# Recurrent gates of a hybrid encoder layer: the array's rows hold one head's high and low part, its columns both gates

## The chip, the cores and the metric

The kernel runs on one core of a Trainium2 chip. The metric is the device time of one execution in microseconds (us), taken as the median of several executions of the same program. A profiled execution gives the trace; its span is the time from the first to the last recorded instruction.

## The reference, cut to what matters

One encoder layer is applied to two sequences of width 1024: a prompt of 512 rows and a sample of 1024 rows. After a LayerNorm the input is multiplied by `w_in` and split into four parts of 512 channels: convolution value and gate, recurrent input and gate. The recurrent half is the part that changes. In each of two directions a depthwise convolution of width 4 gives x, and x goes through a gated linear recurrence with 8 heads of 64 channels:

```python
xh = x.reshape(bsz, seq, RNN_HEADS, RNN_HEAD_DIM)             # 8 heads of 64
gate_a = einsum("bshi,hij->bshj", xh, w_a) + b_a               # 64 x 64 per head
gate_x = einsum("bshi,hij->bshj", xh, w_x) + b_x
r, i = sigmoid(gate_a), sigmoid(gate_x)
log_a = -8 * r * softplus(-lam)
a = exp(log_a);  b = sqrt(-expm1(2 * log_a)) * (i * x)
h[t] = a[t] * h[t-1] + b[t]                                    # or backwards
```

The two directions are added and multiplied by gelu of the recurrent gate. The convolution half is a depthwise convolution of width 31 with a LayerNorm and a swish. Both halves go through `w_out`, a residual and a LayerNorm, and then through a ConvFFN (up to 2 x 2816 channels, convolution of width 3, gelu gate, down to 1024) with a second residual and LayerNorm.

## The kernel before, in words

**Arithmetic.** Every large product is made of three matmuls. An operand is kept as a high part, its rounded copy in the reduced format that the array takes (fp32r), and a low part, the rest. `prod3` (L534) lists the three pairs: high x high, high x low, low x high. `split` (L489) makes the two parts: ScalarE copies the high part, and a second engine (VectorE or GpSimd) subtracts it from the input.

**Layout.** The recurrent channels lie on the 128 partitions in four groups j, two heads in each: head 2j on partitions 0 to 63, head 2j+1 on partitions 64 to 127. A tile of work is 128 channels by 512 columns of time.

**One recurrent chain** is one group j, one direction d and one block of 512 columns (`chain`, L844, for the sample; the loop in `mixer_p`, L777 to L782, for the prompt). It runs `conv4` (one activation and three multiply-adds), `split` with the low part on GpSimd, `rg_gates` (L722), `rg_decay` (L731: five activations with three changes of the activation table, and multiply-adds) and `scan` (L746). In `rg_gates` the weight tile of a gate is a 128 x 128 matrix with the two heads' 64 x 64 blocks on its diagonal and zeros elsewhere. For each of the two gates three matmuls of 128 x 128 by 512 columns go into one PSUM bank, and ScalarE takes a sigmoid of the whole bank; then VectorE multiplies the second gate by x. The banks come from a ring of two.

**Stages and their order.** In the order of the program: LayerNorm and `w_in` of the prompt; `w_in_s`, the same for the sample (16 weight tiles, 48 matmuls each); `mixer_p`, both halves of the prompt's mixer; the prompt's `residual` (192 matmuls with `w_out`) and `ln1`; `mixer_s(1)` and the prompt's `ffn`; then `residual`, `ln1`, `mixer_s(0)` and `ffn(1)` of the second half of the sample; then the same for its first half. `mixer_p` has 8 chains, `mixer_s(1)` 12 (its forward scan runs over both blocks), `mixer_s(0)` 4.

**What sets the order.** The kernel first lists its operations with a cost, a priority and what they depend on. `plan` (L274) simulates the five engines and picks, at each step, the ready operation of the lowest priority number; `look` lets it take an operation that becomes ready within so many ns, `pen` is added to an activation that changes the table. It knows a port that GpSimd and two-input VectorE operations share. `emit` (L356) makes one plan for each entry of `PLANS` (L377) and writes the instructions of every engine in the order of the plan with the shortest end. So every engine has one fixed order, and stages overlap: `w_in_s` (priority 30) fills TensorE beside `mixer_p` (13 to 16), and an `ffn` fills it beside `mixer_s`.

The parameters of the gates are columns of one tile `par` (`C_BA`, `C_BX`, L32 to L34), and the weights are laid out on the host in `layouts` (L1128).

Of the kernel before, what the change touches and what calls it, by code (L numbers as in the profile page):

```python
# [11 lines left out]
AF = mybir.ActivationFunctionType  # L12
ALU = mybir.AluOpType
# [17 lines left out]
C_RB = C_RW + 32  # L31
C_BA = C_RB + 8  # L32
C_BX = C_BA + 8
C_LAM = C_BX + 8  # L34
C_FW = C_LAM + 8
C_FB = C_FW + 3 * 2 * NPAIR
NPAR = C_FB + 2 * NPAIR
# [7 lines left out]
class View:  # L45
# [13 lines left out]
    @property  # L59
    def f32(self):  # L60
        return self._with(lambda a: a.bitcast(F32)) if self.buf.dtype != F32 else self

    @property
    def rev(self):
# [309 lines left out]
                    mybir.DependencyClass.Sync, mybir.DependencyReason.DATA), reason="port")  # L374


PLANS = [(60, 3.0, 0.0, 0), (160, 3.0, 0.0, 0), (160, 8.0, 0.0, 0), (260, 3.0, 0.0, 0)]  # L377


def body(ctx, tc, xp, xs, w_in, gw, w_out, w_up, w_down, par, gb, out_p, out_s):  # L380
# [3 lines left out]
    S = Sched(tc, sb, ps)  # L384
# [23 lines left out]
    col = lambda c: P[c:c + 1]  # L408
# [80 lines left out]
    def split(hi, lo, src, prio, hi_eng="act", lo_eng="dve"):  # L489
        S.copy(hi_eng, hi, src, prio)  # L490
        S.tt(lo_eng, lo, src, hi.f32, ALU.subtract, prio)
# [42 lines left out]
    def prod3(wh, wl, xh, xl):  # L534
        return [(wh, xh), (wh, xl), (wl, xh)]
# [92 lines left out]
    gwt = S.buf("GW", [2, 2, 4, 128], f32r), S.buf("GB", [2, 2, 4, 128], f32r)  # L628
# [35 lines left out]
    def decays():  # L664
# [3 lines left out]
        d = S.buf("sv", [8])  # L668
        lam = P[C_LAM:C_LAM + 8]
        pr = 12  # L670
# [39 lines left out]
    def conv4(src, dst, d, j, n, prio, t0=0, N=None):  # L710
        N = N or n
        order = (3, 2, 1, 0) if d == 0 else (0, 1, 2, 3)
        for i, k in enumerate(order):
# [4 lines left out]
            else:  # L718
                lo, hi = max(t0, -sh), min(t0 + n, N - sh)
                S.stt(dst(lo - t0, hi - t0), src(lo + sh, hi + sh), c, dst(lo - t0, hi - t0), ALU.mult, ALU.add, prio)  # L720

    def rg_gates(xf, hl, r, d, j, banks, prio):  # L722


        for ax, cb in ((0, C_BA), (1, C_BX)):
            bk = S.buf(banks(), [512], psum=True)
            S.mm(bk.all, prod3(gwt[0][d, ax, j], gwt[1][d, ax, j], *hl), True, True, prio)
            S.act(r if ax == 0 else bk.all, bk.all, AF.Sigmoid, 1.0, col(cb + d * 4 + j), prio)
        S.tt("dve", xf, bk.all, xf, ALU.mult, prio)

    def rg_decay(xf, r, q, st, d, j, prio, eng):  # L731

# [33 lines left out]
    def mixer_p():  # L766
        bk = rot(["M2", "M3"])
        acc = S.buf("T3", [4, 512])
        for j, bank in enumerate(("C0", "U2", "U3", "C1")):
            pc = S.buf(bank, [512], psum=True)  # L770
            conv31(lambda a, b: p_c[j, a:b], lambda a, b: pc[a:b], j, 512, 16)
            S.copy("act", acc[j], pc.all, 15)
        for j in range(4):
            t0 = S.buf("T0", [2, 2, 512])
            t1 = S.buf("T1", [2, 2, 512])
            hl = S.buf("G3", [2, 2, 512], f32r)
            for d in range(2):  # L777
                conv4(lambda a, b: p_rx[j, a:b], lambda a, b, d=d: t0[0, d, a:b], d, j, 512, 14)
                split(hl[0, d], hl[1, d], t0[0, d], 14, lo_eng="pool")
                rg_gates(t0[0, d], (hl[0, d], hl[1, d]), t0[1, d], d, j, bk, 14)  # L780
                rg_decay(t0[0, d], t0[1, d], t1[0, d], t1[1, d], d, j, 14, "pool")
                scan(t1[0, d], t0[1, d], t0[0, d], d, 14)  # L782
            S.tt("dve", t1[0, 0], t1[0, 0], t1[0, 1], ALU.add, 14)
            S.tt("dve", t1[0, 0], t1[0, 0], p_ge[j], ALU.mult, 14)
            split(xcP[0][1][j], xcP[1][1][j], t1[0, 0], 14)
        z = S.buf("G1", [4, 512])
        for tt in range(4):
            conv_norm(lambda j: acc[j, tt * 128:(tt + 1) * 128], [(0, 4, z[tt])], tt, "c", bk, 13)
        c = S.buf("T3", [4, 512])
        for j in range(4):  # L790
            b = S.buf(bk(), [512], psum=True)
            S.transposes([(b[tt * 128:(tt + 1) * 128], z[tt, j * 128:(j + 1) * 128]) for tt in range(4)], b.all,
                         idn.all, 13)
            S.act(c[j], b.all, AF.Silu, col(C_CG + j), col(C_CBB + j), 13)
            split(xcP[0][0][j], xcP[1][0][j], c[j], 13)
    mixer_p()


# [45 lines left out]
    def chain(rx, c, hl, d, j, t0, carry, bk, prio):  # L844

        conv4(rx, lambda a, b: c[0, a:b], d, j, 512, prio, t0, N)
        split(hl[0], hl[1], c[0], prio, lo_eng="pool")
        rg_gates(c[0], (hl[0], hl[1]), c[1], d, j, bk, prio)
        rg_decay(c[0], c[1], c[2], c[3], d, j, prio, "pool")
        if carry is not None:  # L850
            e = slice(0, 1) if d == 0 else slice(511, 512)
            S.stt(c[0, e], c[1, e], carry, c[0, e], ALU.mult, ALU.add, prio)
        scan(c[2], c[1], c[0], d, prio)
# [229 lines left out]
    for i in range(4):  # L1083
        for nh in range(2):
            b = S.buf(names(), [512], psum=True)
# [9 lines left out]
        if i == 0:  # L1095
            for nh in range(2):
                b = S.buf(names(), [512], psum=True)
                c = slice(nh * 512, (nh + 1) * 512)
# [9 lines left out]
    q = slice(768, 1024)  # L1108
# [4 lines left out]
    for nh in range(2):  # L1113
        n = 512 - 256 * nh
        v, c = last[nh - 2][0:n], slice(nh * 512, nh * 512 + n)
        x = y0[1][1, c]
        S.stt(v, v, mean, g2(c), ALU.subtract, ALU.mult, 5)
        S.stt(x, v, rstd, b2(c), ALU.mult, ALU.add, 5)
        c = slice(nh * 512, nh * 512 + 512)
        x = y0[1][1, c]  # L1120
# [7 lines left out]
def layouts(i):  # L1128

    c = np.ascontiguousarray  # L1130
    g = {k: np.asarray(v) for k, v in i.items()}
    w_in = c(g["w_in"][0].reshape(8, 128, 16, 128).transpose(2, 1, 0, 3)).reshape(16, 128, 1024)
    w_up = c(g["w_up"][0].reshape(8, 128, 44, 128).transpose(2, 1, 0, 3)).reshape(44, 128, 1024)
    w_out = c(g["w_out"][0].reshape(4, 2, 128, 2, 512).transpose(3, 0, 2, 1, 4)).reshape(2, 4, 128, 1024)
    w_down = c(g["w_down"][0].reshape(22, 128, 1024))
    gw = np.zeros((2, 2, 4, 128, 128), np.float32)
    for ax, n in enumerate(("rg_w_a", "rg_w_x")):
        for d in range(2):
            for h in range(8):
                j, o = divmod(h, 2)  # L1140
                gw[d, ax, j, o * 64:o * 64 + 64, o * 64:o * 64 + 64] = g[n][0, d, h]
    gw = c(gw.transpose(3, 0, 1, 2, 4)).reshape(128, 2048)
    ch = lambda a: a.reshape(-1, 128).T
    par = np.concatenate([
        c(g["conv_dw_w"][0].reshape(CW, 4, 128).transpose(2, 1, 0)).reshape(128, 4 * CW),
        ch(g["conv_dw_b"][0]), ch(g["conv_ln_g"][0]), ch(g["conv_ln_b"][0]),
        ch(g["rnn_conv_w"][0]), ch(g["rnn_conv_b"][0]), ch(g["rg_b_a"][0]), ch(g["rg_b_x"][0]), ch(g["rg_lambda"][0]),
        c(g["ffn_dw_w"][0].reshape(3, 44, 128).transpose(2, 1, 0)).reshape(128, 132), ch(g["ffn_dw_b"][0])], axis=1)
    gb = np.stack([g["ln_in_g"], g["ln_in_b"], g["ln1_g"][0], g["ln1_b"][0], g["ln2_g"][0], g["ln2_b"][0]])
    return {"xp": c(g["x_prompt"][0]), "xs": c(g["x_sample"][0]), "w_in": w_in, "gw": gw, "w_out": w_out, "w_up": w_up,  # L1150
            "w_down": w_down, "par": c(par), "gb": c(gb)}
# [15 lines left out]
```

## Time and profile before

| | before |
|---|---|
| median of 3 executions (lowest to highest) | 1571.3 us (1571.17 to 1571.7) |
| the profiled execution's own time | 1571.57 us |
| its span | 1569.6 us |
| TensorE busy / weight loads busy | 1543.7 us (98%) / 1280.2 us (82%) |
| VectorE busy | 1150.9 us (73%) |
| ScalarE busy | 825.2 us (53%) |
| GpSimd busy | 166.6 us (11%) |
| granted TensorE clock | 0.998 of full speed |

Busy time is the time in which at least one instruction of the engine is open. Matmuls are pipelined and overlap in the record, so a matmul's mean of 390 ns is not what it costs in a row of matmuls; that is read from how many of them start in a stretch of time. PE is TensorE, PEld its weight loads, DVE VectorE, ACT ScalarE, POOL GpSimd and SP the queue that issues the transfers.

### The profile page before, as it was taken

To read this page: it belongs to the slowest core of one execution; us is meant where nothing else is said; L and a number is where in the kernel's file an instruction comes from. 1 tells how busy PE (TensorE), PEld (TensorE's weight loads), DVE (VectorE), ACT (ScalarE), POOL (GpSimd) and SP (SyncE) were. 2 spreads that over 40 slices of the span, in tenths; PEclk is the share of its full clock that TensorE was granted. 3 is DMA by queue.
4 is the path that set the end of the run, shared out by engine and by line. 5 is a ranking of instruction groups with operands and counts; after the bars stand their busy time and mean duration, and the time that the engine had idled before them with its cause. 6 is when DMAs were issued, how large, how long until landed. Compare 5 with 4: busy or idle time off the path is not lost.

```text
span 1569.6 us, 19146 instructions
## 1 busy us (share of the span) xinstructions
PE 1543.7 (98%) x7036; PEld 1280.2 (82%) x7036; DVE 1150.9 (73%) x1849; ACT 825.2 (53%) x1031; POOL 166.6 (11%) x186
## 2 busy tenths in 40 slices
PE   6999999999999999999999999999999999999997
PEld 6888888888887888888887888888888888888885
DVE  8999974589999999653889988744438644545367
ACT  4647885249888883633369634352423433334351
POOL 3101111001211221100211000000002000000003
PEclk9999999999999999999999999999999999999999
DMA  9954337357565467666675766575675666565641
GB/s 375 328 181 139 108 121 239 130 191 227 166 225 183 154 230 234 208 223 220 202 257 181 277 205 210 168 244 191 210 249 184 201 199 199 195 198 178 200 159 67
DMA packets 107661, 316.09 MB, mean 201 GB/s; under 512 B 11952, under 2 KB 12080, under 8 KB 107440
## 3 DMA queue, kind: packets, MB, share of 16 engines
q1 hardware_dynamic: 107568, 314.88, 60.2%
q8 instruction: 55, 0.90, 0.2%
q14 instruction: 38, 0.31, 0.1%
HBM read 247.72 MB, written 67.11 MB: 201 GB/s over the span
## 4 chain that ended last, share of the span: by engine, by line
PE 80%; DVE 11%; ACT 5%; DMA 2%; issue 2%; POOL 0%; SPq 0%; DVEq 0%; ACTq 0%
PE b L262 78%; DVE b L208 7%; ACT b L240 4%; DVE b L199 3%; ACT L240 2%; PE b L270 2%; DMA b<-mixs_d 1%; DVE b L749 0%; DMA lo_up_d<-b 0%; DMA b<-gb 0%; DVE b L430 0%; DMA lo_down_d<-b 0%; POOL b L199 0%; SPq L251 0%; POOL b L222 0%
## 5 line engine op out<-in xcount | busy, mean ns | idle before, releaser
L262 PE MATMUL b<-b,b 128*128 128x512 f32 (+1 forms) x6748 | 1519.2, 386 | 4.3 <-DVE b L199 2.5
L262 PEld LDWEIGHTS b<-b,b 128*128 128x128 f32 x6748 | 1246.7, 188 | 261.7 <-DVE b L199 5.1
L208 DVE SCALAR_TENSOR_TENSOR b<-b,b,b 128x512 f32<-128x512 f32 (+14 forms) x848 | 569.2, 701 | 180.6 <-ACT b L240 167.2
L240 ACT ACTIVATE b<-b 128x1024 fp32r<-128x1024 f32 (+4 forms) x576 | 445.0, 798 | 437.5 <-PE b L262 210.2
L199 DVE TENSOR_TENSOR b<-b,b 128x512 f32<-128x512 f32 (+6 forms) x494 | 394.0, 817 | 144.0 <-ACT b L240 80.7
L240 ACT ACTIVATE b<-b,b 128x512 f32<-128x512 f32 (+2 forms) x346 | 261.3, 775 | 277.6 <-PE b L262 204.6
L199 POOL TENSOR_TENSOR b<-b,b 128x1 f32<-128x1 f32 (+4 forms) x84 | 89.8, 1077 | 1010.0 <-DVE b L222 407.9
L240 ACT ACT_TABLE_LOAD x109 | 139.8, 1283 | 23.5 <-DVE b L208 14.0
L199 POOL TENSOR_TENSOR b<-b 128x512 f32<-128x512 f32 (+1 forms) x47 | 60.8, 1297 | 379.2 <-ACT b L240 190.8
L208 DVE SCALAR_TENSOR_TENSOR b<-b,b 128x512 f32<-128x512 f32 (+2 forms) x81 | 50.8, 640 | 59.9 <-PE b L262 54.6
L430 DVE BATCH_NORM_STATS2 b<-b 128x6 f32<-128x512 f32 x84 | 55.9, 683 | 6.0 <-DMA b<-xp 4.5
L199 DVE TENSOR_TENSOR b<-b 128x1 f32<-128x1 f32 (+3 forms) x85 | 43.2, 525 | 21.2 <-ACT b L240 20.9
L270 PE MATMUL b<-b,b 128*128 128x128 f32 x288 | 39.9, 281 | 11.4 <-DVE b L208 11.4
L208 DVE SCALAR_TENSOR_TENSOR b<-b 128x512 f32<-128x512 f32 (+1 forms) x73 | 48.4, 676 | 0.6 <-ACT b L240 0.5
L270 PEld LDWEIGHTS b<-b,b 128*128 128x128 f32 x288 | 34.8, 145 | 17.1 <-issue 10.9
L749 DVE TENSOR_TENSOR_SCAN b<-b 128x512 f32<-128x512 f32 x24 | 29.1, 1217 | 0.1
L222 POOL TENSOR_SCALAR b<-b 128x1 f32<-128x1 f32 x36 | 15.3, 430 | 7.9 <-DVE b L208 2.3
L222 DVE TENSOR_SCALAR b<-b 128x1 f32<-128x1 f32 (+1 forms) x60 | 8.9, 153 | 1.4 <-POOL b L199 0.9
L432 DVE BATCH_NORM_AGGREGATE b<-b 128x2 f32<-128x12 f32 (+1 forms) x48 | 9.2, 196 | 0.3
L247 DVE COPY b<-b 128x2 f32<-128x2 f32 x44 | 6.6, 150 | 0.0
L222 DVE TENSOR_SCALAR b<-b,b 128x512 f32<-128x512 f32 x2 | 0.9, 483 | 0.0
L437 DVE RECIPROCAL b<-b 128x1 f32<-128x1 f32 x4 | 0.5, 154 | 0.4 <-ACT b L240 0.4
(14 smaller groups left out, 2.2 us busy)
## 6 DMA issues: line engine op xcount, KB each, us to landing
b<-w_up SPq DMA_DIRECT2D x132, 512.0 KB, 4.5
b<-lo_up_d SPq DMA_DIRECT2D x88, 512.0 KB, 4.1
b<-w_down SPq DMA_DIRECT2D x132, 256.0 KB, 4.2
lo_up_d<-b SPq DMA_DIRECT2D x44, 512.0 KB, 5.2
b<-lo_down_d SPq DMA_DIRECT2D x88, 256.0 KB, 3.5
b<-w_in SPq DMA_DIRECT2D x32, 512.0 KB, 5.6
b<-w_out SPq DMA_DIRECT2D x24, 512.0 KB, 4.3
lo_down_d<-b SPq DMA_DIRECT2D x44, 256.0 KB, 5.2
```

The costliest lines, as they stand in the source:

```text
L199: return self.op(eng, cost if eng == "any" else cost[eng], lambda e=eng: self.engine(e).tensor_tensor(out=out(), in0=a(), in1=b(), op=op), ...
L208: o = self.op("dve", cost, lambda: self.nc.vector.scalar_tensor_tensor(out=out(), in0=a(), scalar=s() if isinstance(s, View) else s, in1=b ...
L222: o = self.op(eng, cost, lambda: e.tensor_scalar(out=out(), in0=a(), scalar1=f(s1), scalar2=f(s2), op0=op0, **({"op1": op1} if op1 is not ...
L240: self.nc.scalar.activation(out=out(), in_=a(), func=func, **k)
L247: return self.op("dve", cost, lambda: self.nc.vector.tensor_copy(out(), a()), [a], [out], prio)
L262: self.nc.tensor.matmul(out=out(), lhsT=a(), rhs=b(), start=start and i == 0, stop=stop and i == len(pairs) - 1)
L270: self.nc.tensor.transpose(o(), i(), ident())
L430: S.op("dve", c.n * 1.0417 + 69, lambda i=i, c=c: nc.vector.bn_stats(out=sm_[6 * i:6 * i + 6](), in_=c()), [c], [sm_[6 * i:6 * i + 6]], prio)
L432: S.op("dve", 211, lambda: nc.vector.bn_aggr(out=sm_[12:14](), in_=sm_[0:6 * n]().rearrange("p (a b) -> p a b", a=n)), [sm_[0:6 * n]], [sm ...
L437: S.op("dve", 140, lambda: nc.vector.reciprocal(out=sm_[15:16](), in_=sm_[14:15]()), [sm_[14:15]], [sm_[15:16]], prio)
L749: S.op("dve", out.n * 2.0833 + 69, lambda: nc.vector.tensor_tensor_scan(out=out(), data0=a(), data1=b(), initial=0.0, op0=ALU.mult, op1=AL ...
```

## The change

Each chain's operand is stacked by head. `stack` replaces `split`: the first tile has the high part of head 2j on partitions 0 to 63 and its low part on partitions 64 to 127, the second tile the same for head 2j+1 with the halves exchanged. The high parts are two ScalarE copies of 64 partitions, the low parts one GpSimd and one VectorE subtraction that write to the other half of the partitions. The weight tile of a head has on its columns both gates (64 and 64), and the same 64 x 128 block on its upper and its lower 64 rows. One matmul with the high part of that tile therefore sums high x high and low x high, and one with its low part high x low and low x low: two matmuls per head, four per chain, into one bank per head. A bank then holds both gates of one head, so four sigmoids of 64 partitions bring the gates back to the channels' order; two of them read one half of the partitions and write the other. For that the bias of the second gate is repeated on both halves (`C_BX` takes 16 columns). The list of plans is another one, of twelve.

```diff
-C_LAM = C_BX + 8
+C_LAM = C_BX + 16
...
+    def rows(self, a, b):
+        return self._with(lambda x: x[a:b])
...
-PLANS = [(60, 3.0, 0.0, 0), (160, 3.0, 0.0, 0), (160, 8.0, 0.0, 0), (260, 3.0, 0.0, 0)]
+PLANS = [(look, pen, 0.0, 0) for look in (30, 60, 100, 160) for pen in (3.0, 8.0, 12.0)]
...
+    LOW, HIGH = (0, 64), (64, 128)
+
+    def stack(hl, x, prio):
+        for q, p, w in ((LOW, HIGH, hl[0]), (HIGH, LOW, hl[1])):
+            S.copy("act", w.rows(*q), x.rows(*q), prio)
+            S.tt("pool" if q is LOW else "dve", w.rows(*p), x.rows(*q), w.rows(*q).f32, ALU.subtract, prio)
+
     def rg_gates(xf, hl, r, d, j, banks, prio):
-        for ax, cb in ((0, C_BA), (1, C_BX)):
-            bk = S.buf(banks(), [512], psum=True)
-            S.mm(bk.all, prod3(gwt[0][d, ax, j], gwt[1][d, ax, j], *hl), True, True, prio)
-            S.act(r if ax == 0 else bk.all, bk.all, AF.Sigmoid, 1.0, col(cb + d * 4 + j), prio)
-        S.tt("dve", xf, bk.all, xf, ALU.mult, prio)
+        A, B = (S.buf(banks(), [512], psum=True).all for _ in range(2))
+        for k, bk in enumerate((A, B)):
+            S.mm(bk, [(gwt[0][d, k, j], hl[k]), (gwt[1][d, k, j], hl[k])], True, True, prio)
+        ba, bx = col(C_BA + d * 4 + j), [col(C_BX + (d * 4 + j) * 2 + k) for k in range(2)]
+        S.act(r.rows(*LOW), A.rows(*LOW), AF.Sigmoid, 1.0, ba.rows(*LOW), prio)
+        S.act(A.rows(*LOW), A.rows(*HIGH), AF.Sigmoid, 1.0, bx[0].rows(*LOW), prio)
+        S.act(r.rows(*HIGH), B.rows(*HIGH), AF.Sigmoid, 1.0, ba.rows(*HIGH), prio)
+        S.act(A.rows(*HIGH), B.rows(*LOW), AF.Sigmoid, 1.0, bx[1].rows(*HIGH), prio)
+        S.tt("dve", xf, A, xf, ALU.mult, prio)
...
-                split(hl[0, d], hl[1, d], t0[0, d], 14, lo_eng="pool")
+                stack((hl[0, d], hl[1, d]), t0[0, d], 14)
...
-        split(hl[0], hl[1], c[0], prio, lo_eng="pool")
+        stack(hl, c[0], prio)
...
-    gw = np.zeros((2, 2, 4, 128, 128), np.float32)
-    for ax, n in enumerate(("rg_w_a", "rg_w_x")):
-        for d in range(2):
-            for h in range(8):
-                j, o = divmod(h, 2)
-                gw[d, ax, j, o * 64:o * 64 + 64, o * 64:o * 64 + 64] = g[n][0, d, h]
-    gw = c(gw.transpose(3, 0, 1, 2, 4)).reshape(128, 2048)
+    gw = np.zeros((2, 64, 2, 2, 4, 128), np.float32)
+    for d in range(2):
+        for h in range(8):
+            j, o = divmod(h, 2)
+            m = (g["rg_w_a"][0, d, h], g["rg_w_x"][0, d, h])
+            gw[:, :, d, o, j] = np.concatenate(m if o == 0 else m[::-1], axis=1)
+    gw = gw.reshape(128, 2048)
+    bx = g["rg_b_x"][0].reshape(2, 4, 2, 1, 64)
+    bx = np.broadcast_to(bx, (2, 4, 2, 2, 64)).reshape(16, 128).T
```

## Rows read from the trace of the kernel before

**Rows 1.** The page: span, and busy time (share) xinstructions by engine.

```profile
span 1569.6 us, 19146 instructions
PE 1543.7 (98%) x7036; PEld 1280.2 (82%) x7036; DVE 1150.9 (73%) x1849; ACT 825.2 (53%) x1031; POOL 166.6 (11%) x186
```

**Rows 2.** Busy time in stretches: stretch, length, engine busy (xinstructions), PEclk, DMA share, GB/s.

```profile
160.00:200.00 40.00, 40.00 (x178) 33.10 (x178) 39.68 (x60) 32.18 (x40) 5.19 (x4) 1.00 0.31 106
1280.00:1320.00 40.00, 40.00 (x178) 33.13 (x177) 19.37 (x40) 15.06 (x21) 0.00 (x0) 1.00 0.60 188
```

**Rows 3.** Timeline of PE: start, us, what [idle before <-releaser]; its first and last group.

```profile
10.92 1.94 PE L270 MATMUL b<-b,b 128*128 128x128 f32 x8 [10.92 <-DVE b L208]
...
1534.75 24.64 PE L262 MATMUL b<-b,b 128*128 128x512 f32 x108
```

**Rows 4.** Waits of PE and PEld, 20 to 1550 us: total us, times, longest us.

```profile
PE b L262 <- DVE b L199: 2.5, 4, 1.0
PE b L262 <- ACT b L240: 1.1, 2, 0.8
PE b L262 <- POOL b L199: 0.6, 1, 0.6
...
PEld b L262 <- POOL b L199: 2.6, 5, 1.1
```

**Rows 5.** Groups of instructions, shapes apart: form xcount | busy us, mean ns | idle before.

```profile
L262 PE MATMUL b<-b,b 128*128 128x512 f32 x6508 | 1489.0, 390 | 2.8 <-DVE b L199 1.8 <-POOL b L199 0.6 <-ACT b L240 0.3
...
L240 ACT ACTIVATE b<-b,b 128x512 f32<-128x512 f32 x318 | 231.7, 748 | 240.1 <-PE b L262 204.6 <-DMA b<-mixs_d 9.0 <-DVE b L749 8.8
...
L240 ACT ACTIVATE b<-b 128x512 fp32r<-128x512 f32 x124 | 73.6, 614 | 77.9 <-PE b L270 36.0 <-DVE b L199 20.8 <-POOL b L199 13.0
L199 DVE TENSOR_TENSOR b<-b,b 128x512 fp32r<-128x512 f32 x100 | 66.8, 687 | 12.9 <-ACT b L240 12.5
...
L199 POOL TENSOR_TENSOR b<-b,b 128x512 fp32r<-128x512 f32 x24 | 30.9, 1295 | 153.3 <-ACT b L240 78.3 <-DVE b L208 64.5 <-DVE b L199 10.6
...
L749 DVE TENSOR_TENSOR_SCAN b<-b 128x512 f32<-128x512 f32 x24 | 29.1, 1217 | 0.1
...
L208 DVE SCALAR_TENSOR_TENSOR b<-b,b,b 128x256 f32<-128x256 f32 x2 | 1.0, 478 | 0.0
...
L240 ACT ACTIVATE b<-b,b 128x256 f32<-128x256 f32 x1 | 0.6, 564 | 2.4 <-POOL b L222 2.4
```

**Rows 6.** The chain of waits, in order of time, 110 to 335 us: start, us, what.

```profile
148.01 7.56 DVE b L208 x12
```

**Rows 7.** Busy time in the stages with recurrent chains, columns as in rows 2.

```profile
90.00:220.00 130.00, 130.00 (x575) 107.54 (x574) 129.05 (x191) 89.80 (x112) 15.51 (x12) 1.00 0.39 130
220.00:262.00 42.00, 41.94 (x201) 34.52 (x200) 21.34 (x38) 33.27 (x43) 8.85 (x12) 1.00 0.57 188
335.00:630.00 295.00, 294.32 (x1296) 241.58 (x1295) 287.55 (x397) 227.66 (x280) 56.25 (x42) 1.00 0.62 204
630.00:780.00 150.00, 149.59 (x687) 123.72 (x687) 86.19 (x130) 62.25 (x73) 16.83 (x23) 1.00 0.63 211
```

**Rows 8.** Timeline of the transfer queue SP, 180 to 330 us.

```profile
279.81 0.33 SPq L251 DMA_DIRECT2D b<-w_out  x1
...
285.24 0.33 SPq L251 DMA_DIRECT2D b<-w_out  x1
...
318.09 0.33 SPq L251 DMA_DIRECT2D b<-w_in  x1
```

**Rows 9.** Timeline of PE, 215 to 330 us.

```profile
307.54 3.00 PE L262 MATMUL b<-b,b 128*128 128x512 f32 x12
...
326.29 1.04 PE L270 MATMUL b<-b,b 128*128 128x128 f32 x8
```

**Rows 10.** Timeline of SP, 560 to 860 us.

```profile
656.01 0.80 SPq L251 DMA_DIRECT2D b<-x0s_d  x2
...
703.61 0.33 SPq L251 DMA_DIRECT2D b<-w_out  x1
```

More of the change, by code (lines that the diff above doesn't have):

```diff
@@ L1146, in layouts @@
         ch(g["conv_dw_b"][0]), ch(g["conv_ln_g"][0]), ch(g["conv_ln_b"][0]),
-        ch(g["rnn_conv_w"][0]), ch(g["rnn_conv_b"][0]), ch(g["rg_b_a"][0]), ch(g["rg_b_x"][0]), ch(g["rg_lambda"][0]),
+        ch(g["rnn_conv_w"][0]), ch(g["rnn_conv_b"][0]), ch(g["rg_b_a"][0]), bx, ch(g["rg_lambda"][0]),
         c(g["ffn_dw_w"][0].reshape(3, 44, 128).transpose(2, 1, 0)).reshape(128, 132), ch(g["ffn_dw_b"][0])], axis=1)
```

## The prediction

> **What bounds the kernel now.** I read the busy times first. TensorE is open for 1543.7 of 1569.6 us [rows 1], but an open matmul overlaps its neighbours, so that alone proves little. The second view settles it: the number of TensorE instructions in equal stretches. Beside the prompt's mixer, where VectorE is busy for 39.68 of 40 us, and late in an FFN, where VectorE has half its time free, 178 matmuls start in 40 us [rows 2]. The rate does not depend on what the other engines do, at a granted clock of 1.00, so TensorE runs at its own pace: 40 / 178 = 0.2247 us for each matmul of 128 x 128 by 512 columns. Third, the timeline of TensorE: its first group starts at 10.92 us and its last ends near 1559.4 us [rows 3], so about 21 us are head and tail. Between them the waits for other engines sum to 2.5 + 1.1 + 0.6 = 4.2 us [rows 4]. A time that is won must come out of TensorE's list of work, and what other engines get to do costs nothing until TensorE stands still for it.
>
> **What goes.** There are 24 scans [rows 5], so 24 chains. Each loses two of six matmuls: 48 of the 6508 with 512 columns [rows 5]. The new ones have the same shape as the old (128 rows, 128 columns of weights, 512 columns streamed), so each keeps its 0.2247 us: 48 x 0.2247 = 10.8 us off TensorE, 3.6 in the prompt's mixer (8 chains), 5.4 in `mixer_s(1)` (12) and 1.8 in `mixer_s(0)` (4). Nothing has to be hidden here: in all three stages TensorE has other matmuls to pull forward.
>
> **What comes, per chain.** No row shows an operation on 64 partitions. Above, it costs as much as one on 128 with the same 512 columns; below, as one on 128 with 256 columns, which has as many elements. ScalarE has one copy more (0.614 us) and two sigmoids more (0.748 each): 2.11 us above [rows 5]. Below, with the half-size activation at 0.564 us for each, two copies for one and four sigmoids for two add 0.51 + 0.76 = 1.27 us. VectorE has one subtraction more, 0.687 above and 0.478 below; GpSimd's one subtraction stays, 1.295 us at most [rows 5]. I take the upper values, since all rows of an engine grow with their columns. Over 24 chains that is 51 us for ScalarE and 16.5 us for VectorE. The page "ScalarE: Activation LUTs" of the Trainium skill, section "What ACT_TABLE_LOAD costs", has an activation cost 0.833 ns per column and lane whatever the number of rows; the sum would be the same by it, and no run here shows it yet.
>
> **Order of VectorE's operations.** Twelve multiply-adds in a row take 7.56 us [rows 6], 0.63 each, while such a row's mean is 0.74 in the record: neighbours overlap by 0.1 us. The new subtraction reads partitions 64 to 127, its neighbours start at partition 0. By the page "VectorE: DVE Perf Modes" of the Trainium skill, section "Two Vector instructions with no wait between them", an instruction whose input starts in another group of 32 partitions than the last one's is held until all before it are done, and so is the one behind it. That would cost the overlap twice per chain, 0.2 us, and 4.8 us of VectorE over 24 chains; it would move no term below, because VectorE's time is paid only through a delay for which I leave room.
>
> **Delay of one chain.** r is complete after three sigmoids instead of one: 1.5 us. Ahead of them the second copy and the second subtraction stand beside GpSimd's 1.3 us and then share its port: 0.7 us more. About 2.4 us, by the upper rows, with 0.2 for the fourth matmul.
>
> **Where this lies beside other work.** In the prompt's mixer VectorE is busy for 129.05 of 130 us and then waits on latency (21.34 of 42) [rows 7]. Eight subtractions add 5.5 us, and the last two chains 2.4 us each: the mixer ends between 4 us (five subtractions ahead of its end at the lower price, and no latency) and 12 us later (all, and the shared port against it); I take 8. TensorE meanwhile runs `w_in_s`. How much of that is left? The `w_out` loads come every 5.43 us [rows 8], one per 24 matmuls, so the prompt's residual, 192 matmuls from about 258 us, ends near 301.5 us. From there to the last transposes of `ln1` at 326.29 us [rows 9] TensorE lives on `w_in_s`: 25 matmuls up to 307 us and then groups of 12, 24, 12 and 24 between the transposes, of which the first stands in the rows [rows 9], 97 in all. One more weight tile, loaded at 318.09 us [rows 8], has 48. So the cover is 145 matmuls and the need 97. A delay of 8 us and the 3.6 us saved take 11.6 / 0.2247 = 52 out of it; 93 are left, 4 too few: 0.9 us. At 4 us of delay nothing is missing, at 12 us 21 matmuls, 4.7 us. I take 1.5 us.
>
> In `mixer_s(1)` VectorE has 287.55 of 295 us and gets 12 x 0.687 = 8.2 more, ScalarE 227.66 and gets 25 [rows 7]. VectorE overflows by about 1 us, 3 with the held neighbours; the work slides into the next 150 us, where VectorE is busy for 86 [rows 7]. The FFN's evictions have the better priority numbers (6 against 31), so TensorE is fed first and the mixer slides. Its output was taken up by 656 us, when the residual's second input is loaded into the place of the mixer's result, and the residual's first 24 matmuls were through by 703.61 us [rows 10], so they began near 698: a slack of 42 us against twelve chains with 2.4 us each, 29 us, if none of them overlap. `mixer_s(0)` has only four chains.
>
> Short waits: TensorE's list is written out ahead, so a gate matmul that is planned too early stops it. The 4.2 us of before [rows 4] could go to nothing or double; two operands come late now instead of one, and I take +1.0 us. The twelve plans are judged by the kernel's own table of costs; whichever is taken, only order changes, and that is in these bounds. `par` grows by 8 columns and the gate weights keep their size: nothing.
>
> **Sum.** -10.8 + 1.5 + 1.0 = -8.3 us. The profiled execution took 1571.57 us, 0.27 above the median of 1571.3; from the median the forecast is 1563.0 us. Its own bounds are -10.8 - 4.2 = -15.0 (all waits gone) and -10.8 + 4.7 + 4.2 = -1.9; its core is 1560 to 1567.
>
> **Rivals.**
> 1. The cover of `w_in_s` runs short. If the mixer's end moves by 14 us (ScalarE's additions, 17 us over 8 chains, not hidden behind VectorE), 17.6 us take 78 matmuls, 67 are left, 30 too few: 6.7 us. With 1.0 for waits, 1571.3 - 10.8 + 7.7 = 1568.2 us. For it: VectorE is full in that stage and the chains wait in turn. Against it: ScalarE is at 89.80 of 130 us.
> 2. The order improves. More plans to choose from, fewer table changes at the higher penalty: three of the 4.2 us of waits go as well, 1571.3 - 10.8 - 3.0 = 1557.5 us. For it: ScalarE idles and switches often. Against it: waits of a few tenths lie below what the table of costs resolves.
> 3. Slower: the gates block TensorE. Each chain has two groups of two matmuls, one behind GpSimd's subtraction, one behind VectorE's, where a port is shared. If the table has these too early, TensorE stands at each of them. Five waits of the weight loads for GpSimd took 2.6 us in all before, the longest 1.1 [rows 4]. It decides at 10.8 / 48 = 0.225 us per group; at 0.3 us it costs 14.4, and the time is 1574.9 us. For it: such waits exist. Against it: only 5 in 24 chains, and the table carries latencies for each pair of engines.
> 4. That the change doesn't do what it says would need a gate matmul that costs more than 0.2247 us; four at 0.337 would cost what six did. Shape and type are those of 6508 others, so I give it no share of its own.
>
> **How the numbers follow.** Forecast 0.60, rival 1 0.15, rival 2 0.10, rival 3 0.15. A measurement of this kernel can tell about 0.2% (3.1 us) from no change, so faster means below 1568.2 us. The forecast, rival 2 and most of rival 1 (0.13) are faster: 0.83. The rest of rival 1 (0.02) and the milder part of rival 3 (0.06; 0.16 to 0.29 us per group) give no change, 0.08; the rest of rival 3 is slower, 0.09. The range 1557.0 to 1569.0 us holds the forecast, rival 2 but for its far end, and rival 1 but for its far end: about 8 in 10.
>
> **What would show it.** Right, if the line of L262 has 6700 matmuls instead of 6748, ScalarE about 72 activations and 45 to 55 us more, VectorE 24 instructions more, the quiet stretches still 178 starts in 40 us, and the waits of TensorE stay below 8 us. The step on the cover is wrong if TensorE idles for more than 3 us between the prompt's residual and its FFN; rival 3 is right if waits for GpSimd or VectorE ahead of the gates sum to over 10 us. The price of 64 partitions is read from the new rows directly: 0.6 to 0.75 us on ScalarE if columns count, near 0.56 if elements do. What would make the whole forecast wrong is a stall that no row of before shows: a stage in which TensorE has no other matmul to pull forward.

## The result: slower, and the profile after

The changed kernel takes 1580.14 us in the median (1579.71 to 1581.02), the kernel before beside it 1571.50 us: a ratio of 1.0056 with a 95% interval of 1.0038 to 1.0073. The forecast was 1563.0 us. The profiled execution took 1580.49 us, its span is 1578.4 us and the granted clock 0.997 (0.998 before). A lower clock is a small part of the loss: behind a matmul that started 2.2 us late, TensorE was granted half of full speed (1.2 of 2.4 GHz) from 578.4 to 581.8 us, where matmuls start 0.427 us apart; that is 1.4 us. The trace of before has half speed only in its last 5 us.

The page of the changed kernel, its busy times and one group of instructions (group: form xcount | busy us, mean ns | idle time before). Helpers stand three lines lower than before: L265 issues the matmuls, L243 the activations, L202 the two-input operations and L211 the multiply-adds of VectorE and GpSimd.

```profile
span 1578.4 us, 19184 instructions
PE 1540.4 (98%) x6988; PEld 1270.7 (81%) x6988; DVE 1171.9 (74%) x1875; ACT 887.8 (56%) x1114; POOL 158.3 (10%) x184
...
L265 PE MATMUL b<-b,b 128*128 128x512 f32 (+1 forms) x6700 | 1515.4, 387 | 15.7 <-DVE b L202 8.7
```

Beside [rows 1], TensorE has 48 instructions fewer and is open 3.3 us less, yet the span is 8.8 us longer. The same groups with shapes apart, the new ones among them:

```profile
L243 ACT ACT_TABLE_LOAD x120 | 154.0, 1283 | 22.8 <-DVE b L211 12.4 <-DVE b L435 6.1 <-DVE b L250 2.3
...
L243 ACT ACTIVATE b<-b,b 64x512 f32<-64x512 f32 x96 | 64.0, 667 | 6.5 <-PE b L265 4.5
...
L202 POOL TENSOR_TENSOR b<-b,b 64x512 fp32r<-64x512 f32 x24 | 30.8, 1288 | 162.0 <-ACT b L243 89.6 <-DVE b L202 46.9 <-DVE b L211 24.3
L243 ACT ACTIVATE b<-b 64x512 fp32r<-64x512 f32 x48 | 30.1, 627 | 7.2 <-DVE b L211 6.5
...
L202 DVE TENSOR_TENSOR b<-b,b 64x512 fp32r<-64x512 f32 x24 | 17.0, 714 | 2.6 <-ACT b L243 1.8
```

An operation on 64 partitions has the price of one on 128 with as many columns: the copy 627 ns against 614, the subtractions 714 against 687 on VectorE and 1288 against 1295 on GpSimd [rows 5]. ScalarE also changes its table 11 times more often (120 against 109); which operations bring that was not followed up.

Waits of TensorE and of its weight loads, 20 to 1570 us (total us, times, longest us):

```profile
PEld b L265 <- DVE b L202: 11.9, 15, 1.6
PEld b L265 <- ACT b L243: 10.3, 11, 2.4
PE b L265 <- DVE b L202: 8.7, 15, 1.2
...
PE b L265 <- ACT b L243: 4.0, 5, 1.5
PE b L265 <- DVE b L211: 2.0, 1, 2.0
...
PE b L265 <- POOL b L202: 0.6, 1, 0.6
```

The four lines of PE are 15.3 us, against 4.2 in [rows 4]. They are not all of it, since a matmul also starts late when its weight load waited. So I also took the starts of all matmuls from both traces and summed by how much each distance of more than 0.3 us exceeds the usual 0.227 us (the median distance). That gives 10.8 us in 63 gaps before and 29.4 us in 111 gaps after, the 1.4 us of half speed among them. By stage: the prompt's part up to 345 us 3.7 and 5.6; `mixer_s(1)`, 345 to 720 us, 3.6 and 16.4; 720 to 800 us 0.3 and 0.3; `mixer_s(0)`, 800 to 960 us, 2.2 and 5.9; the rest 1.0 and 1.1. The balance is -48 x 0.227 + 18.6 = +7.7 us of the 8.8 us between the spans; about 1 us lies in smaller differences.

Busy time in stretches of the changed kernel (columns as in rows 2), two quiet ones of its trace and four from the stages with chains beside an FFN:

```profile
160.00:200.00 40.00, 39.97 (x176) 32.40 (x175) 38.86 (x59) 32.23 (x42) 5.61 (x5) 1.00 0.37 121
360.00:400.00 40.00, 39.32 (x171) 31.31 (x170) 38.24 (x52) 39.41 (x49) 6.39 (x5) 1.00 0.66 204
520.00:560.00 40.00, 38.32 (x164) 30.10 (x163) 37.36 (x51) 39.49 (x47) 6.33 (x5) 1.00 0.60 190
840.00:880.00 40.00, 37.87 (x165) 30.43 (x165) 37.85 (x63) 39.40 (x49) 5.15 (x4) 1.00 0.56 182
1280.00:1320.00 40.00, 40.00 (x179) 33.10 (x178) 21.29 (x42) 14.45 (x19) 0.00 (x0) 1.00 0.59 194
345.00:680.00 335.00, 325.32 (x1404) 262.79 (x1403) 324.44 (x442) 274.66 (x338) 56.63 (x43) 0.99 0.63 201
```

The same four of the kernel before:

```profile
360.00:400.00 40.00, 39.61 (x174) 32.17 (x173) 38.68 (x54) 37.65 (x47) 7.67 (x6) 1.00 0.68 210
520.00:560.00 40.00, 39.96 (x177) 32.77 (x176) 39.86 (x55) 35.29 (x42) 7.10 (x6) 1.00 0.54 168
840.00:880.00 40.00, 38.99 (x172) 32.00 (x171) 39.52 (x67) 36.81 (x43) 7.47 (x6) 1.00 0.61 201
...
345.00:680.00 335.00, 333.91 (x1480) 273.90 (x1479) 308.32 (x429) 247.26 (x302) 63.00 (x52) 1.00 0.63 208
```

Late in the FFN TensorE keeps its pace (179 starts in 40 us). Beside the chains it does not: 164 starts where 177 were, and there ScalarE is busy for 39.49 of 40 us. The averages of a long stage hide this: over 335 us ScalarE is at 274.66. The chain of waits of the changed kernel, shares by line of the stretch 520 to 560 us and then of 345 to 680 us (L243 with `b` is an activation, without it a table load):

```profile
by line: ACT b L243 55.7%; ACT L243 32.0%; issue 13.6%; ACTq L243 0.2%
...
by line: PE b L265 29.8%; ACT b L243 28.7%; ACT L243 13.1%; DVE b L211 11.1%; issue 7.0%; DVE b L202 6.9%; DVE b L766 1.7%; DMA b<-w_down 1.6%; SPq L254 0.3%; ACTq L243 0.1%; DVEq L202 0.0%; DVEq L211 0.0%
```

And the first of the two in the kernel before:

```profile
by line: PE b L262 100.5%; issue 0.1%
```

There the chain ran through TensorE alone. Now it runs through ScalarE, so what ScalarE loses in this stretch can be paid in time; `f_all` below tries it. What it loses stands in the timeline of ScalarE, changed kernel (start us, length us, what):

```profile
376.39 0.68 ACT L243 ACTIVATE b<-b,b 64x512 f32<-64x512 f32 x1
376.98 1.56 ACT L243 ACTIVATE b<-b 128x1024 fp32r<-128x1024 f32 x2
378.45 0.76 ACT L243 ACTIVATE b<-b,b 128x512 f32<-128x512 f32 x1
379.11 1.05 ACT L243 ACTIVATE b<-b 128x1024 fp32r<-128x1024 f32 x1
380.19 1.36 ACT L243 ACTIVATE b<-b,b 64x512 f32<-64x512 f32 x2
381.57 1.06 ACT L243 ACTIVATE b<-b 128x1024 fp32r<-128x1024 f32 x1
382.66 1.46 ACT L243 ACTIVATE b<-b,b 128x512 f32<-128x512 f32 x2
```

Subtract each end from the next start. After 376.39 (a sigmoid that reads and writes partitions 0 to 63) the next activation starts 0.09 us before the recorded end; so do the two behind it. At 380.19 come two sigmoids, of which the first reads from partition 64 on and the second reads and writes there: 379.11 + 1.05 = 380.16, so they start 0.03 after the end, and the next one, back at partition 0, starts at 381.57, 0.02 after 381.55. (At 382.66 such a distance stands without a change of partition.) Over the whole trace neighbours overlap by 0.098 us, and where the start partition of input or output changes, the second starts 0.025 after the first's end: 0.123 us lost. The kernel before has 18 pairs of neighbours with such a small positive distance (5 to 45 ns), the changed one 129, of which 105 stand at a change of the start partition by the kernel's written order; the 111 more are worth 13.7 us of ScalarE.

VectorE around the new subtraction, changed kernel:

```profile
353.04 2.07 DVE L211 SCALAR_TENSOR_TENSOR b<-b,b,b 128x509 f32<-128x509 f32 x3
355.19 0.69 DVE L202 TENSOR_TENSOR b<-b,b 64x512 fp32r<-64x512 f32 x1
355.91 4.71 DVE L211 SCALAR_TENSOR_TENSOR b<-b,b,b 128x512 f32<-128x512 f32 x7
```

It starts 0.08 us after the one ahead of it, and its follower 0.03 after its end; where nothing is held, neighbours overlap by 0.08. Of the 24 such subtractions 18 start 0.031 us after the one ahead, and 19 followers 0.031 to 0.033 after them: 0.11 us for each held operation. The page "VectorE: DVE Perf Modes" of the Trainium skill, section "Two Vector instructions with no wait between them", foretells both holds, and the trace agrees. The same place in `f_all`, a run below in which the subtraction takes all 128 partitions, in the same order of work:

```profile
351.67 1.41 DVE L211 SCALAR_TENSOR_TENSOR b<-b,b,b 128x512 f32<-128x512 f32 x2
353.03 0.69 DVE L202 TENSOR_TENSOR b<-b,b 128x512 fp32r<-128x512 f32 x1
353.64 4.70 DVE L211 SCALAR_TENSOR_TENSOR b<-b,b,b 128x512 f32<-128x512 f32 x7
```

Here 353.03 + 0.69 = 353.72, and the next starts at 353.64.

### The profile page after: what moved, and what is told of

Its sections match the earlier page's. It is cut to its first block, busy times and chain, and to the rows that moved or that the text cites. A ratio compares the mean times of both kernels' runs of the same rounds, so it can differ in the third digit from the quotient of the medians.

```text
span 1578.4 us, 19184 instructions
## 1 busy us (share of the span) xinstructions
PE 1540.4 (98%) x6988; PEld 1270.7 (81%) x6988; DVE 1171.9 (74%) x1875; ACT 887.8 (56%) x1114; POOL 158.3 (10%) x184
## 4 chain that ended last, share of the span: by engine, by line
PE 70%; ACT 14%; DVE 9%; issue 3%; DMA 3%; POOL 0%; SPq 0%; DVEq 0%; ACTq 0%; POOLq 0%
PE b L265 69%; ACT b L243 10%; DVE b L211 6%; ACT L243 4%; DVE b L202 3%; PE b L273 2%; DMA b<-mixs_d 1%; DVE b L766 1%; DMA b<-w_in 1%; DMA b<-hf_d 0%; DMA b<-gb 0%; POOL b L202 0%; DMA b<-w_down 0%; DMA b<-lo_down_d 0%; SPq L254 0%
## 5 line engine op out<-in xcount | busy, mean ns | idle before, releaser
L265 PE MATMUL b<-b,b 128*128 128x512 f32 (+1 forms) x6700 | 1515.4, 387 | 15.7 <-DVE b L202 8.7
L265 PEld LDWEIGHTS b<-b,b 128*128 128x128 f32 x6700 | 1237.2, 188 | 279.2 <-DVE b L202 11.9
L211 DVE SCALAR_TENSOR_TENSOR b<-b,b,b 128x511 f32<-128x511 f32 (+13 forms) x848 | 568.5, 702 | 170.8 <-ACT b L243 157.6
L243 ACT ACTIVATE b<-b 128x1024 fp32r<-128x1024 f32 (+5 forms) x600 | 459.9, 791 | 415.3 <-PE b L265 206.9
L202 DVE TENSOR_TENSOR b<-b,b 128x512 f32<-128x512 f32 (+5 forms) x519 | 412.7, 814 | 124.1 <-ACT b L243 65.5
L243 ACT ACTIVATE b<-b,b 128x512 f32<-128x512 f32 (+3 forms) x394 | 294.8, 762 | 246.8 <-PE b L265 179.7
L202 POOL TENSOR_TENSOR b<-b,b 128x1 f32<-128x1 f32 (+4 forms) x83 | 87.2, 1058 | 1015.1 <-DVE b L225 524.1
L211 DVE SCALAR_TENSOR_TENSOR b<-b,b 128x512 f32<-128x512 f32 (+2 forms) x81 | 50.8, 643 | 66.7 <-PE b L265 53.7
L202 POOL TENSOR_TENSOR b<-b 128x512 f32<-128x512 f32 (+1 forms) x46 | 59.5, 1294 | 396.3 <-ACT b L243 209.0
L433 DVE BATCH_NORM_STATS2 b<-b 128x6 f32<-128x512 f32 x84 | 56.0, 684 | 10.9 <-PE b L273 5.9
L202 DVE TENSOR_TENSOR b<-b 128x512 f32<-128x512 f32 (+3 forms) x86 | 44.0, 528 | 24.5 <-ACT b L243 23.8
L211 DVE SCALAR_TENSOR_TENSOR b<-b 128x512 f32<-128x512 f32 (+1 forms) x73 | 49.7, 687 | 3.0 <-ACT b L243 2.9
L273 PE MATMUL b<-b,b 128*128 128x128 f32 x288 | 40.0, 281 | 12.1 <-DVE b L211 11.4
L273 PEld LDWEIGHTS b<-b,b 128*128 128x128 f32 x288 | 34.7, 145 | 17.9 <-issue 10.9
L225 POOL TENSOR_SCALAR b<-b 128x1 f32<-128x1 f32 x36 | 10.4, 293 | 2.6
```

The costliest lines, as they stand in the source:

```text
L202: return self.op(eng, cost if eng == "any" else cost[eng], lambda e=eng: self.engine(e).tensor_tensor(out=out(), in0=a(), in1=b(), op=op), ...
L211: o = self.op("dve", cost, lambda: self.nc.vector.scalar_tensor_tensor(out=out(), in0=a(), scalar=s() if isinstance(s, View) else s, in1=b ...
L225: o = self.op(eng, cost, lambda: e.tensor_scalar(out=out(), in0=a(), scalar1=f(s1), scalar2=f(s2), op0=op0, **({"op1": op1} if op1 is not ...
L243: self.nc.scalar.activation(out=out(), in_=a(), func=func, **k)
L265: self.nc.tensor.matmul(out=out(), lhsT=a(), rhs=b(), start=start and i == 0, stop=stop and i == len(pairs) - 1)
L273: self.nc.tensor.transpose(o(), i(), ident())
```

## The experiments

Theory A: the saving on TensorE is real, and it is eaten by the additions on ScalarE and VectorE, mostly by operations held at a changed start partition, which the kernel's table of costs does not have, so that TensorE's fixed order runs into operands that are not there yet. Its rivals are named in the expectations. "Its table's end" is the end that the kernel's own planner gave the order in use. Each run's ratio is to the kernel before measured beside it, with its 95% interval. The gap sums are those of above.

**The held operations alone.** In three kernels the order stays that of the changed kernel, since an operation's price in the table depends on its columns only, and 64-row operations become 128-row operations that start at partition 0.

```diff
# f_all: both edits; f_sig: the sigmoids alone; f_stack: copies and subtractions alone
-S.act(A.rows(*LOW), A.rows(*HIGH), AF.Sigmoid, 1.0, bx[0].rows(*LOW), prio)
+S.act(A, A, AF.Sigmoid, 1.0, bx[0], prio)      # the other three likewise
...
-S.copy("act", w.rows(*q), x.rows(*q), prio)
+S.copy("act", w, x, prio)
-S.tt("pool" if q is LOW else "dve", w.rows(*p), x.rows(*q), w.rows(*q).f32, ALU.subtract, prio)
+S.tt("pool" if q is LOW else "dve", w, x, w.f32, ALU.subtract, prio)
```

> The changed kernel with its order of instructions kept on every engine, but every copy, subtraction and sigmoid on 64 partitions widened to all 128, so that none starts at partition 64 (the halves are therefore not exchanged: the gates' values are left out). Number, columns and order of the instructions stay. Theory (holds): in the trace of the changed kernel ScalarE's neighbours overlap by about 98 ns, but stand 25 ns apart where one of them starts at another partition, 123 ns lost at each of some 111 places, 13.7 us, and VectorE loses about 113 ns at some 44 places, 5 us; the table of costs does not know them, so the written order is late and TensorE stands still. Without them the time falls to 1563 to 1567 us. Rival (load): ScalarE and VectorE are simply full beside the FFN by the 72 activations and 24 subtractions more; these stay, so the time stays at 1576 to 1580 us.

> As the run with all widened, but only the four sigmoids of a chain are widened to 128 partitions (their halves are not exchanged); the copies and subtractions stay as in the changed kernel. Theory (holds): most of ScalarE's holds go, about 80 of 111, some 10 of 13.7 us, VectorE's stay: 1567 to 1572 us. Rival (load): 1578 to 1580 us.

> As the run with all widened, but only the two copies and two subtractions of a chain are widened to 128 partitions (what they stack is left out); the sigmoids stay as in the changed kernel. Theory (holds): a third of ScalarE's holds and all of VectorE's go: 1572 to 1577 us. Rival (load): 1578 to 1580 us.

Measured: `f_all` 1569.19 us, 0.9979 (0.9970 to 0.9989); `f_sig` 1572.56, 1.0002 (0.9992 to 1.0011); `f_stack` 1578.44, 1.0034 (1.0022 to 1.0045). With the same number and length of operations, in the same order, the whole loss turns into a small gain. So the start partitions cost 1580.1 - 1569.2 = 10.9 us in this order, the sigmoids' 7.6 alone; taken against the kernel before beside each run, 11.9, and 8.5 and 2.6 for the two parts. Held pairs on ScalarE (neighbours 5 to 45 ns apart): 11, 48, 101 (129 in the changed kernel); gap sums 18.0, 21.2 and 27.4 us (29.4). `f_all` and `f_sig` are 2.2 and 0.6 us slower than the theory had at most, and `f_stack` lies where the rival had it: the copies and subtractions account for little.

How full ScalarE is does not tell the kernels apart. Two stretches of `f_all` and its chain of waits in the second:

```profile
360.00:400.00 40.00, 39.99 (x176) 32.68 (x175) 39.22 (x56) 39.71 (x50) 8.50 (x7) 1.00 0.72 227
520.00:560.00 40.00, 39.54 (x171) 31.42 (x170) 37.84 (x52) 39.69 (x49) 6.48 (x5) 1.00 0.67 213
...
by line: ACT b L243 53.6%; ACT L243 29.0%; issue 12.0%; DVE b L211 4.8%; DVE b L202 1.5%; ACTq L243 0.2%
```

ScalarE is as busy as in the changed kernel and the chain runs through it as well, but 50 and 49 of its instructions start in these stretches where 49 and 47 did, and 176 and 171 matmuls where 171 and 164 did.

**A table that knows more.**

```diff
# e_costs: price of an operation that writes 64 rows
-cost = out.n / 1.2 + (51 if a.psum else 93) + 90 * len(ptr)
+cost = out.n / 1.2 + (51 if a.psum else 93) + 90 * len(ptr) + (120 if getattr(out, "part", False) else 0)
...
+# VectorE's two-input operations: + 115
```

> The changed kernel with one edit in the planner's table: an activation on 64 partitions costs 120 ns more and a VectorE subtraction on 64 partitions 115 ns more, about what the trace shows for them; instructions stay the same, the order is planned anew. Theory (the order is stale because the table is short): with the true prices the written order fits the chip again, the waits of TensorE fall from 15.7 to under 8 us and the time to 1568 to 1574 us. Rival (load): the prices were not the matter, 1577 to 1582 us.

Measured: 1582.08 us, 1.0058 (1.0043 to 1.0073), with 137 held pairs. That is where the rival had it. With this table the twelve plans bring no gain: the best order had an end at 1572.0 us, and the chip took 10 us more than that. This run also has the lowest clock: 1580.1 us at 0.996 up to 1584.1 us at 0.991, and three stretches of its trace, 17 us in all, at half speed, in which 8.2 of its 32.2 us of gaps lie. Whether the old table misled the planner is therefore not settled by it.

**The two sides of the change apart.**

```diff
# e_mm: kernel before, a gate's third product left out
-S.mm(bk.all, prod3(gwt[0][d, ax, j], gwt[1][d, ax, j], *hl), True, True, prio)
+S.mm(bk.all, prod3(gwt[0][d, ax, j], gwt[1][d, ax, j], *hl)[:2], True, True, prio)
# e_before_adds: kernel before, six matmuls; sigmoid, copy and subtraction in two halves each
+for q in ((0, 64), (64, 128)):
+    S.act((r if ax == 0 else bk.all).rows(*q), bk.all.rows(*q), AF.Sigmoid, 1.0, col(cb + d * 4 + j).rows(*q), prio)
...
# e_oldplans: changed kernel with the list PLANS of before
```

> The kernel before with only the 48 matmuls taken out: each gate leaves out its third product (low weights by high input), and nothing else is changed. Theory A (the change's saving on TensorE is real, and what comes after it eats it): 48 x 0.2247 = 10.8 us faster, about 1561.6 us (1559 to 1565), waits of TensorE near the 4.2 us of before. Rival B (the saving is not to be had: the chains of VectorE and ScalarE set the end of the mixers, TensorE only waits longer): 1567 to 1572 us, waits of TensorE 8 us or more.

> The kernel before with only the change's additions: per chain each of the two sigmoids, the copy and the subtraction is done in two operations on partitions 0 to 63 and 64 to 127; six matmuls stay. Theory A (the additions cost about 19 us: some 11 for operations held at a new start partition and some 8 for the extra operations on full engines): 1572.4 + 19 = 1591 us, 1585 to 1596. Rival C (they cost only because TensorE has fewer matmuls left to run beside the mixers): below 1580 us. The planner's own table, without the held operations, puts this one's end 3.9 us after the kernel before.

> The changed kernel with the four old plans to choose from; its table then sees an end at 1567.9 us instead of 1562.4. If the held operations cost in any order (theory A): 14 to 20 us over its table, 1582 to 1588 us. If the loss hangs on the one order that was chosen (rival D): 1576 us or less.

Measured: `e_mm` 1564.45 us, 0.9950 (0.9935 to 0.9965): 7.8 us gained (5.5 to 10.2), short of theory A's 10.8 and far from rival B. Its gap sum is 14.2 us, 3.4 more than before, and 10.9 - 3.4 = 7.5. So the matmuls are worth their price, but about a third of it goes into later starts; that TensorE, with less to do, reaches its operands earlier would explain this, but the order is a new one too and the two are not told apart. `e_before_adds` 1587.00 us, 1.0093 (1.0078 to 1.0108): the additions cost 14.8 us with all six matmuls in place (19 expected), so rival C falls. The two sides sum to +7.0 us, near the change's +8.6. `e_oldplans` 1588.55 us, 1.0103 (1.0087 to 1.0120), 20.7 over its table's end: a second order loses as well, so rival D falls as it was put. That every order loses is not shown, and two orders below do not.

**Which order.** `e_costs_90` is `e_costs` with `PLANS = [(90, 8.0, 0.0, 0)]`, whose end by the table is 1562.6 us.

> The changed kernel, with 0.12 us more in the table for each ScalarE and 0.115 for each VectorE operation on 64 partitions, and the plan (look 90, penalty 8) that this table puts at 1562.6 us instead of 1572.0. If the lag of the chip on the table stays what it was with that table (10 us): 1573 us, near the kernel before. If it was that one order that ran badly: 1563 to 1567 us. If the order does not matter and the additions cost what they cost: 1580 us.

Measured: 1570.76 us, 0.9993 (0.9983 to 1.0002), 8.2 us over its table's end. The same operations as in `e_costs` in another order are 11.3 us faster, with 139 held pairs. So the 10.9 us are the price of the holds in the order of the changed kernel, not in any. Orders matter as much as the whole change: its own operations took between 1570.8 us here and 1588.6 us in `e_oldplans`.

**A version of the two findings, and its controls.** Each copy may as well take all partitions, since the subtraction writes over the wrong half; the subtractions leave VectorE.

```diff
# v_pool_aware
-S.copy("act", w.rows(*q), x.rows(*q), prio)
-S.tt("pool" if q is LOW else "dve", w.rows(*p), x.rows(*q), w.rows(*q).f32, ALU.subtract, prio)
+S.copy("act", w, x, prio)
+S.tt("pool", w.rows(*p), x.rows(*q), w.rows(*q).f32, ALU.subtract, prio)
...
+cost += 0 + (HELD[e] if at_part[e] != o.part else 0)      # in plan(): act 123 ns, dve 113 ns
+PLANS = [(76, 1.0, 0.0, 0)]
# v_aware: plan() as above and 6 ns for each operation, no other edit; PLANS = [(60, 8.0, 0.0, 0)]
# e_before_72: kernel before, PLANS = [(72, 8.0, 0.0, 0)]
```

> A version of the changed kernel: the copies take all 128 partitions (the other half is written over by the subtraction afterwards, so its result is the same), both subtractions are on GpSimd, and the kernel's table adds 0.123 us on ScalarE and 0.113 on VectorE wherever an operation starts at another partition than the one before it; plan (look 76, penalty 1). Its table's end: 1561.4 us. Every kernel with 48 matmuls fewer has run 5 to 9 us over a table that knows of the held operations, so theory A expects 1566.5 to 1570 us, faster than before by 0.1 to 0.4%. If two subtractions in a row on GpSimd delay the gates (1.3 us more per chain): 1575 us or more, waits of TensorE over 12 us.

> The changed kernel's own operations, with a table that knows the held operations as in v_pool_aware and adds 6 ns to each operation of ScalarE and VectorE; plan (look 60, penalty 8). The table's end: 1567.7 us. If the table is now complete, as theory A has it: 1568 to 1571 us, ScalarE still with 100 or more held pairs, and waits of TensorE under 10 us. If the table lacks something else: 1575 us or more.

> Control: the kernel before with another plan (look 72, penalty 8), whose end by the table is 1567.3 us instead of 1570.2. If a better plan is to be had for the kernel before as well, 1569 us. If the plan of before merely ran close to its table (1.8 us over it) and others do not: 5 to 7 us over its table, 1572 to 1574 us.

Measured: `v_pool_aware` 1566.68 us, 0.9972 (0.9962 to 0.9983), faster than both kernels. `v_aware` 1571.75, 0.9996 (0.9987 to 1.0005), with 139 held pairs: an order made with the holds known brings the time back to that of before, a little slower than expected, with waits of TensorE of 11.1 us instead of under 10. Over the end by the table in use the times are 17.7, 20.7 and 12.9 us where operations are held that the table does not know (the changed kernel, `e_oldplans`, `e_before_adds`), 4.0 to 10.1 where it knows them (`v_aware`, `v_pool_aware`, `e_costs_90`, `e_costs`), and 1.3 and 6.8 where few are held (the kernel before, `f_all`). `e_before_72` 1569.81, 0.9987 (0.9978 to 0.9996): 2.3 us of a gain are to be had by an order for the kernel before too. Against that control the version keeps 1569.8 - 1566.7 = 3.1 us by the medians, but the two intervals overlap, so this rest is not clear of the noise. Page of `v_pool_aware`:

```profile
span 1564.2 us, 19174 instructions
PE 1534.0 (98%) x6988; PEld 1270.7 (81%) x6988; DVE 1154.8 (74%) x1851; ACT 880.6 (56%) x1110; POOL 187.4 (12%) x208
```

and its stretches 520 to 560 and 345 to 680 us, with its chain of waits by line in the longer one:

```profile
520.00:560.00 40.00, 37.57 (x165) 30.32 (x164) 38.67 (x51) 37.22 (x47) 12.76 (x10) 1.00 0.60 188
...
345.00:680.00 335.00, 328.15 (x1440) 268.25 (x1439) 327.58 (x444) 273.44 (x339) 73.47 (x56) 1.00 0.63 205
```

```profile
by line: PE b L273 61.4%; ACT b L251 16.6%; ACT L251 7.4%; DVE b L219 4.9%; issue 3.7%; DVE b L210 2.8%; DMA b<-w_up 1.7%; POOL b L210 1.6%; DVE b L778 0.4%; PE b L281 0.3%; POOLq L210 0.0%; ACTq L251 0.0%
```

1440 matmuls start where the changed kernel had 1404, and VectorE is back near its busy time of before. TensorE is 61% of the chain instead of 30%, but that share does not follow the time: it is 28.8% in `f_all` and 36.5% in `e_before_72`, which is faster than the kernel before with 70.1%. 104 held pairs are left on ScalarE, since the sigmoids still move between halves.

## Why the prediction was wrong

**The step that failed** is the term for short waits, +1.0 us on 4.2 us that "could go to nothing or double", and the sentence ahead of it: "The FFN's evictions have the better priority numbers (6 against 31), so TensorE is fed first and the mixer slides." Measured, the gaps grew by 18.6 us, 12.8 of them in `mixer_s(1)`; and the 4.2 us were not all of the waiting to begin with: by the distances it was 10.8 us. A priority decides only while the order is being written. On the chip ScalarE and VectorE work off a fixed list, and when they run late by the holds, the FFN's evictions in that list are late with them. By the kernels' written order, the gaps at full clock grew from 4.2 to 15.1 us at matmuls of the FFN and from 3.0 to 8.5 us at those of the gates, so the stall is mainly not at the gates.

How the 18.6 us come about is shown in parts: 3.4 with the matmuls gone and nothing added (`e_mm`), 7.2 with the extra operations and no holds (`f_all`), 18.6 with the holds (1.4 of them at half speed). The first two differ in their order of work too, so the 3.8 us between them are less certain than the 11.4 of the holds, which were taken in one order.

**Point by point.**
- 48 matmuls at 0.2247 us: right in count (6700) and price (179 starts in the quiet stretch). Alone they bring 7.8 us.
- 64 partitions priced by columns: right. ScalarE's busy time grew by 62.6 us instead of 45 to 55; 14.1 us of it are the 11 table loads, which I had not counted. VectorE grew by 21.0 us and 26 instructions instead of 16.5 and 24.
- Held operations: foreseen on VectorE at 0.2 us per chain, measured 0.11 for each of two; not foreseen on ScalarE, where there are more of them. That it "would move no term" is the second error, and it has the same root: I took ScalarE for free in `mixer_s(1)` at 227.66 of 295 us [rows 7], while a stretch of 40 us was already at 37.65 before.
- Cover of `w_in_s`: 1.5 us were taken and none was lost, by luck. The last transposes of the prompt's `ln1` start 14.9 us later than in [rows 9], later than the 4 to 12 us foreseen allow, and by the sum that would have cost 4 us or more. But the cover was larger too: by the written order 108 matmuls of `w_in_s`, and not 48, stood behind these transposes before, and the need was 84 and not 97, since the residual ran up to 304.2 us. 36 are left, and TensorE has no gap there:

```profile
324.78 0.60 PE L273 MATMUL b<-b,b 128*128 128x128 f32 x4
325.14 3.02 PE L265 MATMUL b<-b,b 128*128 128x512 f32 x12
...
341.17 1.03 PE L273 MATMUL b<-b,b 128*128 128x128 f32 x8
341.96 8.42 PE L265 MATMUL b<-b,b 128*128 128x512 f32 x36
```

- Slack of `mixer_s(1)`: its first transposes for the convolution half's norm moved from 629.05 us to 690.90 us, more than the 29 us at most that I had reckoned and the 42 us of slack [rows 10], and still 720 to 800 us has no more gaps than before. The loss lies inside the stage and not behind it.
- Rival 3 (slower) had the right sign, but its mechanism only in part. Waits of PE for VectorE and GpSimd sum to 11.3 us over all matmuls; the sign that I had set was 10 us ahead of the gates alone, and there the gaps are 8.5 us, whatever was waited for. I had given it a chance of 0.15.

## What to carry to other kernels

Count the start partitions that an edit brings to ScalarE and VectorE, since each change cost 0.11 to 0.12 us here, once there and once on the way back, and write whole tiles where the surplus is written over anyway. Where the order is fixed beforehand, a priority does not protect the bound engine: look at its feeders in stretches of 40 us and not over a stage. Such a stretch shows where to look, not what is lost: with ScalarE busy for 39.49 us 164 matmuls started, with 39.69 us 171 (`f_all`), and with 37.22 us 165 (`v_pool_aware`). Compare an edit with more than one order of both kernels before a gain or loss of under 1% is put down to the edit.

## What the runs showed of the hardware that was not expected

ScalarE also waits for the end of the activation ahead of it where input or output starts at another partition: 0.025 us after its recorded end instead of 0.098 before it, at 64-row operations that start at partition 64 and at most of their followers, not at those that start at 0. In the changed kernel none of the 84 that start at 64, in input or output, and elsewhere than the one ahead overlaps it; of the 37 that follow them at partition 0 three do, each behind a sigmoid that read from 64 and wrote to 0. The page "ScalarE: Activation LUTs" of the Trainium skill, section "What ACT_TABLE_LOAD costs", gives an overlap of about 93 ns for activations back to back; this trace has 98.

The granted clock fell to half for 3.4 or 6.8 us between 100 us and the last 20 us of eight of the thirteen traces, each time behind late matmuls (one by 2.2 us in the changed kernel, one by 5.6 us in `e_costs_90`), and not in the kernel before, `f_all`, `e_mm`, `v_pool_aware` and `e_before_72`. Matmuls of 512 columns then started 0.427 us apart instead of 0.227, so a stall of TensorE can be paid a second time.
